# The last round of a hybrid decoder by 272 and 240 tokens, with a fixed order of both norms' work

## The chip, the cores and the metric

The kernel runs on one core of one Trainium2 chip. The metric is the device time of one execution in microseconds (us). A core has five engines that run their own instruction queues in order: TensorE (PE, with its weight loads PEld), VectorE (DVE), ScalarE (ACT), GpSimd (POOL) and SyncE (SP, which here issues DMAs only). They wait for one another by semaphores.

## The reference

Two layers of a decoder trunk. Each is an RMSNorm, one projection for two groups of heads (attention with forgetting, and retention), an output projection with a residual add, then a second RMSNorm and a SwiGLU feed-forward block with a residual add. 16 learned meta tokens stand before the 512 real ones and are dropped at the end, after a final RMSNorm.

```python
def rmsnorm(x, g):
    x32 = x.astype(jnp.float32)
    y = x32 * lax.rsqrt(jnp.mean(x32 * x32, axis=-1, keepdims=True) + EPS)
    return (y * g.astype(jnp.float32)).astype(x.dtype)
...
    hn = rmsnorm(h, ffn_norm_g)
    ff = jax.nn.silu(jnp.einsum('bld,df->blf', hn, w_gate)) * jnp.einsum('bld,df->blf', hn, w_up)
    return h + jnp.einsum('blf,fd->bld', ff, w_down)
...
    for i in range(DEPTH):
        h = hybrid_layer(h, ...)
    h = rmsnorm(h, final_norm)
    return h[:, N_META:]
```

D_MODEL is 1024, the feed-forward width 2816, everything float32.

## The kernel before

**Layout.** The residual stream is eight tiles `h[0]` to `h[7]`, each 128 features by 528 tokens (16 meta and 512 real); the second layer computes its feed-forward block for the 512 real tokens alone, columns 16 to 528. Each weight block of 128 features by up to eight blocks is fetched by SP, and split on the chip into a high part (`whi`, `fwhi`, rounded to fp32r) and a low part (`wlo`, `fwlo`); activations are split the same way (`ah`, `al`). A product is then three fp32r matmuls: high by high, low by high, high by low.

**The feed-forward block** (`ffn`) goes in rounds over the 22 blocks of the hidden width (`ROUNDS`); each round's part of the down projection is added to `h` (`down`). The last round has three hidden blocks (n = 3). In the second layer (`last`) its down projection is written out in `ffn` itself, from `add_part` on: the tokens go in two parts, `LC`, of 320 and 192 columns, and for each part the eight feature blocks m one after the other. One such product is 3 x 3 = 9 matmuls into one bank of PSUM (`psum_a`, four banks in turn), and `add_part` (L1010) adds the bank to `h[m]` on VectorE.

**The final norm** needs the sum over all 1024 features of the squares, so over all eight tiles. For the first part `squares` (L308 to L314) squares each tile on ScalarE and sums the squares on VectorE, `col_parts` splits the sum into a high and a low part (`sqh`, `sql`, L128, L129), and `col_rstd` multiplies both by a matrix of ones on TensorE (L273), which sums over the 128 partitions and spreads the result. From it come 1/rms by a logarithm (L278) and an exponential (L279) on ScalarE and one Newton step of three instructions on VectorE (L280, L282, L283). `scaled` (L1066) multiplies each tile by the norm's weight on ScalarE, `final` (L1053) multiplies two tiles at a time by 1/rms on VectorE and has SP write them out (L1056). For the second part `squares_last` (L323 to L336) does the same with the squares of the last two tiles going to the sums by themselves: tile 6 as float32, tile 7 split into two.

**Order.** A list of steps, `steps`, is put together first and then run; `merge` puts the steps in `places` between those of `rnd` by the index of a product's step (`end` is the end of the first part). TensorE's instructions stand in exactly this order. The instructions of the other engines are ordered by a scheduler, except those that `tc.keep_in_program_order` pins; `tc.high_priority` moves others forward. Before, `places` has ten entries: all of the first part's squares and scalings behind its last product, its 1/rms nine steps later (behind the third product of the second part), everything else behind the last product:

```python
            LC = ((t0, t0 + 320), (t0 + 320, T))
...
            places = [(end, lambda: squares(fin[0], LC[0:1])),
                      (end + 9, lambda: rstd(fin[0], LC[0:1], "r")),
                      (end + 9, lambda: scaled(fin[0], *LC[0], 0, NK)),
                      (2 * end, lambda: scaled(fin[1], *LC[1], 0, NK - 1)),
...
                      (2 * end, lambda: final(fin[1], *LC[1], 0, NK))]
```

GpSimd does subtractions of the weight splits in the attention stages (L177) and nothing after them.

Of the kernel before, what the change touches and what calls it, by code (L numbers as in the profile page):

```python
# [10 lines left out]
F32 = mybir.dt.float32  # L11
F32R = mybir.dt.float32r
AF = mybir.ActivationFunctionType
ALU = mybir.AluOpType

D = 1024
NK = D // 128
SEQ = 512
META = 16
T = SEQ + META  # L20
# [8 lines left out]
HB = NK // 2  # L29
EPS = 1e-6  # L30
# [8 lines left out]
def hybrid_kernel(ctx, tc, x_t, w_in, w_fl, w_out, w_gate, w_up, w_down, vecs, b_fg, rope, decay, mask, ident, out_t):  # L39
    nc = tc.nc  # L40
# [9 lines left out]
    h = [state.tile([128, T], F32, name=f"h{k}") for k in range(NK)]  # L50
# [9 lines left out]
    ones = const.tile([128, 128], F32R, name="ones")  # L60
    nc.vector.memset(ones.bitcast(F32), 1.0)
    epsc = const.tile([128, 1], F32, name="epsc")
# [64 lines left out]
    def split(hi, lo, src):  # L127
        nc.scalar.copy(hi, src)  # L128
        nc.vector.tensor_sub(lo, src, hi.bitcast(F32))  # L129
# [109 lines left out]
    def psum():  # L239
        return psd.tile([128, 2, 512], F32, name="psd", tag="psd")  # L240

    def psum_a():
        return psa.tile([128, 512], F32, name="psa", tag="psa")
# [5 lines left out]
    def tt(name, dt=F32):  # L249
        tag, bufs = tags[name]  # L250
        return tmp.tile([128, T], dt, name=name, tag=tag, bufs=bufs)
# [4 lines left out]
    def fft(tag, dt=F32R, shape=(128, T), bufs=None):  # L256
        return phase["ffn"].tile(list(shape), dt, name=tag, tag=tag, bufs=bufs)

    def col_parts(src, cols):
        c_all = slice(cols[0][0], cols[-1][1])  # L260
        sh = tt("sqh", F32R)
        sl = tt("sql", F32R)
        split(sh[:, c_all], sl[:, c_all], src[:, c_all])
        return sh, sl

    def col_rstd(parts, n, cols, rname):


        c_all = slice(cols[0][0], cols[-1][1])
        views = [psum_a()[:, 0:c1 - c0] for c0, c1 in cols]  # L270
        for i, s in enumerate(parts):
            for v, (c0, c1) in zip(views, cols):
                nc.tensor.matmul(v, ones if s.dtype == F32R else ones.bitcast(F32), s[:, c0:c1], start=(i == 0), stop=(i == len(parts) - 1))  # L273
        with tc.high_priority():
            r = tt(rname)
            a = tt("nwt")
            for v, (c0, c1) in zip(views, cols):
                nc.scalar.activation(r[:, c0:c1], v, AF.Ln, bias=epsc, scale=1.0 / n)  # L278
            nc.scalar.activation(r[:, c_all], r[:, c_all], AF.Exp, scale=-0.5)  # L279
            nc.vector.tensor_mul(a[:, c_all], r[:, c_all], r[:, c_all])  # L280
            for v, (c0, c1) in zip(views, cols):
                nc.vector.scalar_tensor_tensor(a[:, c0:c1], v, n * EPS, a[:, c0:c1], ALU.add, ALU.mult)  # L282
            nc.vector.scalar_tensor_tensor(r[:, c_all], a[:, c_all], 3.0 * n, r[:, c_all], ALU.subtract, ALU.mult)  # L283
        return r
# [18 lines left out]
    def squares(st, cols, pinned=False):  # L303
        c = slice(cols[0][0], cols[-1][1])
        acc = tt("ss")
        for k in range(NK):
            if k == 0:
                first = nc.scalar.activation(acc[:, c], h[0][:, c], AF.Square)  # L308
                if pinned:
                    tc.keep_in_program_order(first)  # L310
            else:
                sq = tt("sq")
                nc.scalar.activation(sq[:, c], h[k][:, c], AF.Square)
                nc.vector.tensor_add(acc[:, c], acc[:, c], sq[:, c])  # L314
        st["parts"] = col_parts(acc, cols)

    def squares_last(st, cols):

        c = slice(*cols[0])
        acc = tt("ss")  # L320
        for k in range(NK - 2):
            sq = tt("sq") if k else acc
            nc.scalar.activation(sq[:, c], h[k][:, c], AF.Square)  # L323
            if k:
                with tc.high_priority():
                    nc.vector.tensor_add(acc[:, c], acc[:, c], sq[:, c])
        hi, lo = col_parts(acc, cols)
        one = fft("S", F32, (128, T), 2)
        t = fft("tl1", shape=(128, 2, T))
        sh, sl = t[:, 0], t[:, 1]  # L330
        sq = tt("sq")
        nc.scalar.activation(one[:, c], h[NK - 2][:, c], AF.Square)
        nc.scalar.activation(sh[:, c], h[NK - 1][:, c], AF.Square)
        with tc.high_priority():
            nc.vector.tensor_mul(sq[:, c], h[NK - 1][:, c], h[NK - 1][:, c])
            nc.vector.tensor_sub(sl[:, c], sq[:, c], sh[:, c].bitcast(F32))  # L336
        st["parts"] = (hi, one, lo, sh, sl)

    def rstd(st, cols, rname="R"):

        st["R"] = col_rstd(st["parts"], D, cols, rname)
# [394 lines left out]
    def ffn(l, st, real, last):  # L736
        QC = REAL if real else FULL
        t0 = META if real else 0
        w = (T - t0) // 2
# [90 lines left out]
        class Unit:  # L830
# [42 lines left out]
            def bank(self, n):  # L873
                def go():
                    if n not in self.t:
                        if n == "x":
                            self.t["x"] = psum_a()
                        else:
                            ps = self.t["zy"] = psum()
                            self.t["z"], self.t["y"] = ps[:, 0], ps[:, 1]  # L880
                    return self.t[n]
                return go
# [89 lines left out]
        for r, (f0, f1) in enumerate(ROUNDS):  # L972
            for f in range(f0, f1):
# [12 lines left out]
                if fills:  # L986
                    p, g0, g1 = fills.pop(0)
# [12 lines left out]
        n = f1 - f0  # L1000
        js = [down_job(p, f0, f1) for p, _, _ in fills]
        if not last:
            for p in range(NK // 2):
                for s in range(2):
                    steps += down(js[p], s, 2 * p + s, f0, f1, False)
        else:

            def add_part(m, c0, c1, bank):
                def go():
                    nc.vector.tensor_add(h[m][:, c0:c1], bank()[:, 0:c1 - c0], h[m][:, c0:c1])  # L1010
                return go

            rnd = []
            LC = ((t0, t0 + 320), (t0 + 320, T))
            for c0, c1 in LC:
                for m in range(NK):
                    ps = []

                    def bank(ps=ps):
                        if not ps:  # L1020
                            ps.append(psum_a())
                        return ps[0]

                    rnd += product(js[m // 2], m % 2 * n, lambda k, c0=c0, c1=c1: [t[:, c0:c1] for t in acts[f0 + k]],
                                   bank, True, True, n, add_part(m, c0, c1, bank))
            fin = [{}, {}]
            end = NK * n
            places = [(end, lambda: squares(fin[0], LC[0:1])),
                      (end + 9, lambda: rstd(fin[0], LC[0:1], "r")),
                      (end + 9, lambda: scaled(fin[0], *LC[0], 0, NK)),  # L1030
                      (2 * end, lambda: scaled(fin[1], *LC[1], 0, NK - 1)),
                      (2 * end, lambda: squares_last(fin[1], LC[1:2])),
                      (2 * end, lambda: final(fin[0], *LC[0], HB, NK)),
                      (2 * end, lambda: scaled(fin[1], *LC[1], NK - 1, NK)),
                      (2 * end, lambda: final(fin[0], *LC[0], 0, HB)),
                      (2 * end, lambda: rstd(fin[1], LC[1:2], "R")),
                      (2 * end, lambda: final(fin[1], *LC[1], 0, NK))]
            steps += merge(rnd, places)
        for i in range(HB):
            steps.insert(NK + 4 + 9 * i, x_forms(i))  # L1040
# [4 lines left out]

    gf = const.tile([128, NK], F32, name="gf")
    nc.vector.tensor_scalar_mul(gf, vec[:, V_FIN:V_FIN + NK], RSC)

    def final(st, c0, c1, k0, k1):
        r = st["R"][:, c0:c1].unsqueeze(1).broadcast_to([128, 2, c1 - c0])  # L1050
        for k in range(k0, k1, 2):
            y = st["y"][k // HB][:, k % HB:k % HB + 2]
            mul = nc.vector.tensor_mul(y, y, r)  # L1053
            if k0:
                tc.keep_in_program_order(mul)
            nc.sync.dma_start(out_t[k:k + 2, :, c0 - META:c1 - META].rearrange("k p c -> p k c"), y)  # L1056

    def scaled(st, c0, c1, k0, k1):
        if k0 == 0:
            if c0 == META:  # L1060
                st["y"] = [fft(f"th{i}", F32, (128, HB, c1 - c0)) for i in range(2)]
            else:
                y = fft("tl0", F32, (128, NK, c1 - c0))
                st["y"] = [y[:, 0:HB], y[:, HB:NK]]
        for k in range(k0, k1):
            y = nc.scalar.activation(st["y"][k // HB][:, k % HB], h[k][:, c0:c1], AF.Copy, scale=gf[:, k:k + 1])  # L1066
            if k0:
                tc.keep_in_program_order(y)

    def layer(l):  # L1070

# [155 lines left out]
```

## Time and profile before

| | us |
|---|---|
| median of 3 runs | 1300.8 (1298.96 to 1301.67) |
| the profiled execution | 1302.07 |
| its span, first to last instruction | 1300.3 |

The profile is of one execution. Its first page gives the span, the busy time of each engine and the costliest groups of instructions; further views give the busy time in windows, the instructions in order of time, and the chain of waits: from the last instruction back to what released it at each step. A row of the timeline has the start, the duration, the engine, the line of the kernel, the operation, what is written from what, the shape, a count of merged instructions, and in brackets how long the engine was idle before and what ended that. `h<-psa,h` is the residual add, `th<-h,gf` and `tl<-h,gf` are the scalings of the first and second part, `ss<-ss,sq` the summing of squares, `tl<-tl,R` the products with 1/rms of the second part. SPq is SP's queue of DMA issues.

### The profile page before, as it was taken

How to read it: one execution, taken by the hardware profiler on the slowest of the kernel's cores; microseconds unless marked ns; L12 is line 12 of the kernel's file. 1: busy time of each engine (PE TensorE's matmuls, PEld its weight loads, DVE VectorE, ACT ScalarE, POOL GpSimd, SP SyncE). 2: the span in 40 equal slices, each digit the busy share in tenths (PEclk: the TensorE clock that was granted, in tenths of full speed). 3: DMA queues.
4: the chain of work that ended last, by engine and by line, in shares of the span. 5: the costliest groups of instructions: out<-in, count | busy, mean ns of one | idle time of the engine just before them, and what ended most of it. 6: DMA issues, size and time to landing. Idle time of an engine off the chain costs nothing.

```text
span 1300.3 us, 23291 instructions
## 1 busy us (share of the span) xinstructions
PE 1271.6 (98%) x9326; PEld 1210.3 (93%) x9326; DVE 1005.5 (77%) x1827; ACT 706.7 (54%) x1277; POOL 192.7 (15%) x157
## 2 busy tenths in 40 slices
PE   8999999999999999999999999999999999999996
PEld 7999999999999999999998989988789999999995
DVE  7877756869988777777786767568899888888866
ACT  6776555576444444444466665457764444444444
POOL 3332333230000000000013324333200000000000
PEclk9999899999999999999999999999999999999998
DMA  5322222213333333332323222222224333333321
GB/s 196 107 76 72 74 82 82 60 55 122 103 110 98 98 98 98 98 98 82 102 71 115 74 82 82 77 87 66 97 81 129 99 98 97 98 111 103 96 65 65
DMA packets 45468, 120.54 MB, mean 93 GB/s; under 512 B 5376, under 2 KB 12032, under 8 KB 45360
## 3 DMA queue, kind: packets, MB, share of 16 engines
q1 hardware_dynamic: 45120, 118.90, 29.1%
q8 instruction: 73, 1.20, 0.4%
q14 instruction: 35, 0.29, 0.1%
q0 software_dynamic: 96, 0.13, 0.1%
q10 hardware_dynamic: 144, 0.02, 0.0%
HBM read 116.91 MB, written 2.13 MB: 92 GB/s over the span
## 4 chain that ended last, share of the span: by engine, by line
PE 82%; DVE 9%; ACT 6%; issue 1%; DMA 1%; POOL 0%; SPq 0%; DVEq 0%; ACTq 0%; POOLq 0%
PE psd L200 23%; PE psa L823 17%; PE psd L958 14%; PE psd L823 13%; PE psa L200 5%; PE psa L958 4%; PE psa L396 2%; PE psa L480 1%; PE psa L687 1%; PE psa L540 1%; DVE xl L299 1%; ACT whi L176 1%; PE psa L657 1%; DVE tq L585 1%; DVE ptl L129 1%
## 5 line engine op out<-in xcount | busy, mean ns | idle before, releaser
L177 POOL TENSOR_TENSOR wlo<-raw,whi 128x512 fp32r<-128x512 f32 x136 | 186.8, 1388 | 399.5 <-ACT whi L176 396.6
L200 PE MATMUL psd<-xh,whi 128*128 128x264 f32 (+1 forms) x792 | 198.0, 318 | 5.1 <-ACT whi L176 4.7
L200 PE MATMUL psd<-xh,wlo 128*128 128x264 f32 (+1 forms) x792 | 188.1, 305 | 0.4 <-POOL wlo L177 0.4
L200 PE MATMUL psd<-xl,whi 128*128 128x264 f32 (+1 forms) x792 | 188.0, 305 | 0.0
L200 PEld LDWEIGHTS psd<-xh,whi 128*128 128x128 f32 x792 | 130.2, 192 | 9.6 <-ACT whi L176 4.7
L200 PEld LDWEIGHTS psd<-xh,wlo 128*128 128x128 f32 x792 | 128.7, 191 | 6.5 <-POOL wlo L177 0.6
L200 PEld LDWEIGHTS psd<-xl,whi 128*128 128x128 f32 x792 | 129.3, 191 | 4.2 <-DVE xl L299 0.3
L176 ACT CAST whi<-raw 128x512 fp32r<-128x512 f32 (+1 forms) x170 | 99.6, 613 | 34.4 <-issue 17.8
L811 ACT CAST whi<-raw 128x1024 fp32r<-128x1024 f32 (+2 forms) x62 | 54.9, 885 | 49.8 <-PE psd L823 37.5
L811 ACT CAST fwhi<-raw 128x1024 fp32r<-128x1024 f32 (+2 forms) x62 | 55.7, 898 | 47.4 <-PE psd L823 39.7
L812 DVE TENSOR_TENSOR wlo<-raw,whi 128x1024 fp32r<-128x1024 f32 (+2 forms) x62 | 62.8, 1013 | 11.5 <-ACT whi L811 11.4
L812 DVE TENSOR_TENSOR fwlo<-raw,fwhi 128x1024 fp32r<-128x1024 f32 (+2 forms) x62 | 63.9, 1031 | 9.0 <-ACT fwhi L811 8.6
L823 PE MATMUL psa<-tl,whi 128*128 128x264 f32 (+1 forms) x232 | 65.8, 284 | 0.0
L823 PE MATMUL psa<-th,whi 128*128 128x264 f32 (+1 forms) x232 | 65.8, 284 | 0.0
L823 PE MATMUL psa<-th,wlo 128*128 128x264 f32 (+1 forms) x232 | 65.7, 283 | 0.0
L823 PE MATMUL psa<-th,fwhi 128*128 128x264 f32 (+1 forms) x224 | 63.6, 284 | 0.0
L823 PE MATMUL psa<-th,fwlo 128*128 128x264 f32 (+1 forms) x224 | 63.5, 283 | 0.0
L823 PE MATMUL psa<-tl,fwhi 128*128 128x264 f32 (+1 forms) x224 | 63.4, 283 | 0.0
L499 ACT ACTIVATE pdNone<-pdNone,nmax 128x144 f32<-128x144 f32 (+1 forms) x64 | 37.0, 577 | 47.9 <-DVE nmax L486 35.7
L129 DVE TENSOR_TENSOR ptl<-psa,pth 128x512 fp32r<-128x512 f32 (+4 forms) x88 | 41.8, 490 | 23.3 <-ACT pth L128 23.1
L811 ACT CAST fwhi<-S 128x1024 fp32r<-128x1024 f32 x20 | 21.0, 1051 | 69.7 <-PE psa L823 66.3
L889 ACT COPY e<-psa 128x264 f32<-128x264 f32 (+1 forms) x114 | 42.8, 375 | 27.7 <-PE psa L823 23.8
(311 smaller groups left out, 4035.7 us busy)
## 6 DMA issues: line engine op xcount, KB each, us to landing
raw<-w_in SPq DMA_DIRECT2D x54, 512.0 KB, 3.5
raw<-w_gate SPq DMA_DIRECT2D x44, 512.0 KB, 3.9
fraw<-w_up SPq DMA_DIRECT2D x38, 512.0 KB, 3.5
raw<-w_down SPq DMA_DIRECT2D x64, 256.0 KB, 2.9
raw<-w_out SPq DMA_DIRECT2D x16, 512.0 KB, 3.6
raw<-w_down SPq DMA_DIRECT2D x32, 192.0 KB, 2.5
bc<-cdr SPq DMA_DIRECT2D x16, 264.0 KB, 3.5
raw<-w_up SPq DMA_DIRECT2D x6, 512.0 KB, 3.4
```

What stands on the lines that cost most here:

```text
L129: nc.vector.tensor_sub(lo, src, hi.bitcast(F32))
L176: nc.scalar.copy(hi, job["raw"][:, c0:c1])
L177: sub(lo, job["raw"][:, c0:c1], hi.bitcast(F32))
L200: nc.tensor.matmul(ps[1][b][:, 0:c1 - c0], w[:, wk, :], x[:, c0:c1], start=(k == 0 and i == 0), stop=(k == n - 1 and i == 2))
L299: nc.vector.scalar_tensor_tensor(xl[:, c], h[k][:, c], g, xh[:, c].bitcast(F32), ALU.mult, ALU.subtract)
L396: nc.tensor.transpose(ps[:, 128 * j:128 * j + 128], src[:, o:o + 128], idt)
L499: nc.scalar.activation(pr, pr, AF.Exp, bias=nmax[0:nq], scale=-1.0, accum_out=rsum)
L811: nc.scalar.copy(hi, src)
L812: nc.vector.tensor_sub(lo, src, hi.bitcast(F32))
L823: nc.tensor.matmul(bank()[:, 0:b.shape[-1]], a[:, o + k, :], b, start=(fresh and k == 0 and i == 0), stop=(k == n - 1 and i == 2), skip_gr ...
L889: nc.scalar.copy(self.t["e"][:, i], self.t["x"][:, 0:w])
L958: nc.tensor.matmul(v[:, 0:c1 - c0], a[:, s * n + k, :], b[:, c0:c1], start=(k == 0 and i == 0), stop=(k == n - 1 and i == 2))
```

## The change

The functions `squares_last`, `final` and `scaled` go. The last round's tokens are parted by 272 and 240 (`PA`, `PB`). What follows each product of the second part is written out by hand in `after_0` to `after_7`, and nearly all of it is pinned to that order on VectorE and ScalarE; `after_a` follows the first part's last product. 1/rms of the first part is computed between the products of the second (`root` on ScalarE in `after_2`, `newton` on VectorE in `after_3` and `after_4`). The squares of the second part's tiles 1 to 4 are added to that of tile 0 as before; those of tiles 5, 6 and 7 go to the sums on TensorE as float32 by themselves, so five operands are summed: three in float32, and the high and the low part of the sum of tiles 0 to 4. The products with 1/rms of the first part's tiles 0 to 3 (two instructions of 544 columns) and of the second part's tiles 6 and 7 (one of 480) are on GpSimd, the other five on VectorE. The order of SP's output DMAs is: first part 0, 2, 4, 6, then second part 6, 0, 2, 4.

```diff
-            LC = ((t0, t0 + 320), (t0 + 320, T))
-            for c0, c1 in LC:
+            PA, PB = (t0, t0 + 272), (t0 + 272, T)
+            ca, cb = slice(*PA), slice(*PB)
+            na, nb = PA[1] - PA[0], PB[1] - PB[0]
+            fin = {}
...
+                    f = nc.vector.tensor_add(h[m][:, c0:c1], bank()[:, 0:c1 - c0], h[m][:, c0:c1])
+                    if c0 > t0:
+                        pin(f)
...
+            for c0, c1 in (PA, PB):
...
-            fin = [{}, {}]
+            def scale_a(m):
+                nc.scalar.activation(fin["ya"][m // HB][:, m % HB], h[m][:, ca], AF.Copy, scale=gf[:, m:m + 1])
+
+            def scale_b(*ms):
+                for m in ms:
+                    pin(nc.scalar.activation(fin["yb"][:, m], h[m][:, cb], AF.Copy, scale=gf[:, m:m + 1]))
+
+            def square_b(m):
+                if m == 0:
+                    t = fft("S", F32, (128, 6, w), 2)
+                    fin["one"] = [t[:, i, 0:nb] for i in range(3)]
+                    fin["acc"], fin["rb"], fin["tb"] = (t[:, i, 0:nb] for i in range(3, 6))
+                    d = fin["acc"]
+                elif m < NK - 3:
+                    fin["sq", m] = d = tt("sq")[:, 0:nb]
+                else:
+                    d = fin["one"][m - NK + 3]
+                pin(nc.scalar.activation(d, h[m][:, cb], AF.Square))
+
+            def sum_b(m):
+                pin(nc.vector.tensor_add(fin["acc"], fin["acc"], fin["sq", m]))
+
+            def out(eng, y, r, k, c0, c1):
+                pair = r.unsqueeze(1).broadcast_to([128, 2, c1 - c0])
+                f = eng.tensor_mul(y, y, pair)
+                if eng is nc.vector:
+                    pin(f)
+                nc.sync.dma_start(out_t[k:k + 2, :, c0 - META:c1 - META].rearrange("k p c -> p k c"), y)
+
+            def out_a(eng, k):
+                out(eng, fin["ya"][k // HB][:, k % HB:k % HB + 2], fin["ra"], k, *PA)
+
+            def out_b(eng, k):
+                out(eng, fin["yb"][:, k:k + 2], fin["rb"], k, *PB)
+
+            def root(r, v):
+                pin(nc.scalar.activation(r, v, AF.Ln, bias=epsc, scale=1.0 / D))
+                pin(nc.scalar.activation(r, r, AF.Exp, scale=-0.5))
+
+            def newton(i, r, v, a):
+                if i == 0:
+                    pin(nc.vector.tensor_mul(a, r, r))
+                elif i == 1:
+                    pin(nc.vector.scalar_tensor_tensor(a, v, D * EPS, a, ALU.add, ALU.mult))
+                else:
+                    pin(nc.vector.scalar_tensor_tensor(r, a, 3.0 * D, r, ALU.subtract, ALU.mult))
+
+            def sums(v, parts):
+                for i, t in enumerate(parts):
+                    nc.tensor.matmul(v, ones if t.dtype == F32R else ones.bitcast(F32), t, start=(i == 0), stop=(i == len(parts) - 1))
+
+            def after_a():
...
+                for m in range(NK):
+                    sq = tt("sq") if m else acc
+                    nc.scalar.activation(sq[:, ca], h[m][:, ca], AF.Square)
+                    if m:
+                        nc.vector.tensor_add(acc[:, ca], acc[:, ca], sq[:, ca])
+                    scale_a(m)
+                hi, lo = tt("sqh", F32R), tt("sql", F32R)
+                nc.scalar.copy(hi[:, ca], acc[:, ca])
...
+            def after_0():
+                hi, lo, acc = fin["a"]
+                pin(nc.vector.tensor_sub(lo, acc, hi.bitcast(F32)))
+                square_b(0)
+
+            def after_1():
+                square_b(1)
+
+            def after_2():
+                fin["va"] = psum_a()[:, 0:na]
+                sums(fin["va"], fin["a"][0:2])
...
+                root(fin["ra"], fin["va"])
+                sum_b(1)
+                square_b(2)
+
+            def after_3():
+                a = fin["ra"], fin["va"], fin["ta"]
+                sum_b(2)
+                newton(0, *a)
+                newton(1, *a)
+                square_b(3)
+                scale_b(0, 1)
+
+            def after_4():
+                newton(2, fin["ra"], fin["va"], fin["ta"])
+                sum_b(3)
+                square_b(4)
+                scale_b(2)
+                out_a(nc.gpsimd, 0)
+                out_a(nc.gpsimd, 2)
+
+            def after_5():
+                sum_b(4)
+                scale_b(3)
+                square_b(5)
+                hi, lo = tt("sqh", F32R)[:, 0:nb], tt("sql", F32R)[:, 0:nb]
+                pin(nc.scalar.copy(hi, fin["acc"]))
+                fin["b"] = hi, lo
+
+            def after_6():
+                square_b(6)
+
+            def after_7():
+                hi, lo = fin["b"]
+                pin(nc.vector.tensor_sub(lo, fin["acc"], hi.bitcast(F32)))
+                square_b(7)
+                scale_b(4)
+                v = psum_a()[:, 0:nb]
+                sums(v, (fin["one"][0], hi, fin["one"][1], lo, fin["one"][2]))
+                root(fin["rb"], v)
+                out_a(nc.vector, 4)
+                out_a(nc.vector, 6)
+                scale_b(5, 6, 7)
+                for i in range(3):
+                    newton(i, fin["rb"], v, fin["tb"])
+                out_b(nc.gpsimd, 6)
+                for k in (0, 2, 4):
+                    out_b(nc.vector, k)
+
             end = NK * n
-            places = [(end, lambda: squares(fin[0], LC[0:1])),
...
+            places = [(end, after_a)] + [(end + n * (i + 1), f) for i, f in enumerate(
+                (after_0, after_1, after_2, after_3, after_4, after_5, after_6, after_7))]
```

More of the change, by code (lines that the diff above doesn't have):

```diff
@@ L315, in squares @@
         st["parts"] = col_parts(acc, cols)
[L317 to L337, printed above, removed]
     def rstd(st, cols, rname="R"):
@@ L1006, in ffn, with pin @@
         else:
+            def pin(f):
+                tc.keep_in_program_order(f)
+            PA, PB = (t0, t0 + 272), (t0 + 272, T)
+            ca, cb = slice(*PA), slice(*PB)
+            na, nb = PA[1] - PA[0], PB[1] - PB[0]
+            fin = {}
             def add_part(m, c0, c1, bank):
                 def go():
-                    nc.vector.tensor_add(h[m][:, c0:c1], bank()[:, 0:c1 - c0], h[m][:, c0:c1])
+                    f = nc.vector.tensor_add(h[m][:, c0:c1], bank()[:, 0:c1 - c0], h[m][:, c0:c1])
+                    if c0 > t0:
+                        pin(f)
                 return go
             rnd = []
-            LC = ((t0, t0 + 320), (t0 + 320, T))
-            for c0, c1 in LC:
+            for c0, c1 in (PA, PB):
                 for m in range(NK):
@@ L1025, in ffn @@
                                    bank, True, True, n, add_part(m, c0, c1, bank))
-            fin = [{}, {}]
-            end = NK * n
-            places = [(end, lambda: squares(fin[0], LC[0:1])),
[L1029 to L1037, printed above, removed]
+            def scale_a(m):
+                nc.scalar.activation(fin["ya"][m // HB][:, m % HB], h[m][:, ca], AF.Copy, scale=gf[:, m:m + 1])
@@ new lines, in sums @@
+            def sums(v, parts):
+                for i, t in enumerate(parts):
+                    nc.tensor.matmul(v, ones if t.dtype == F32R else ones.bitcast(F32), t, start=(i == 0), stop=(i == len(parts) - 1))
+            def after_a():
+                fin["ya"] = [fft(f"th{i}", F32, (128, HB, na)) for i in range(2)]
+                fin["yb"] = fft("tl0", F32, (128, NK, nb))
+                acc = tt("ss")
+                for m in range(NK):
[6 more added lines that the diff above has]
+                nc.scalar.copy(hi[:, ca], acc[:, ca])
+                fin["a"] = (hi[:, ca], lo[:, ca], acc[:, ca])
@@ new lines, in after_0 @@
+            def after_0():
[7 more added lines that the diff above has]
+                sums(fin["va"], fin["a"][0:2])
+                fin["ra"], fin["ta"] = (fft("e", F32, (128, T), 2)[:, 0:na] for _ in range(2))
+                root(fin["ra"], fin["va"])
+                sum_b(1)
+                square_b(2)
@@ L1047, in hybrid_kernel @@
     nc.vector.tensor_scalar_mul(gf, vec[:, V_FIN:V_FIN + NK], RSC)
[L1049 to L1068, printed above, removed]
     def layer(l):
```

## The prediction

> **What bounds the kernel now.** I read the page first, then the windows by stage, then the chain of waits, and the timelines only of the last 35 us: the compiled instructions of both kernels are the same on every engine, with the same waits, up to the last round, so only that stretch can change.
>
> ```profile
> span 1300.3 us, 23291 instructions
> PE 1271.6 (98%) x9326; PEld 1210.3 (93%) x9326; DVE 1005.5 (77%) x1827; ACT 706.7 (54%) x1277; POOL 192.7 (15%) x157
> ```
>
> ```profile
> 1286.50:1289.60 3.10, 0.00 (x0) 0.00 (x0) 1.17 (x4) 1.76 (x5) 0.00 (x0) 1.00 0.30 111
> 1289.60:1296.20 6.60, 2.13 (x6) 1.64 (x6) 5.63 (x14) 2.09 (x7) 0.00 (x0) 0.50 0.27 99
> 1296.20:1298.70 2.50, 0.00 (x0) 0.00 (x0) 0.48 (x2) 0.00 (x0) 0.00 (x0) 0.50 0.95 312
> ```
>
> TensorE bounds the kernel at 98% of the span, but not its end. The columns of the windows are PE, PEld, DVE, ACT, POOL, granted clock, DMA share and GB/s. TensorE has no matmul between 1286.5 and 1289.6, only six matmuls, the sums of the norm, after that, and from 1296.2 to 1298.7 only the output moves, with the DMA engines at 95%. The last 13.8 us are a tail of VectorE, ScalarE and DMA. The chain of waits says what they wait for:
>
> ```profile
> 1286.42 0.28 DVE h L1010
> 1286.70 0.02 issue
> 1286.73 0.45 ACT tl L1066
> 1287.18 0.26 ACT sq L323
> 1287.44 0.02 issue
> 1287.46 0.36 DVE ss L326
> 1287.82 0.28 DVE h L1010
> ...
> 1290.00 0.28 DVE h L1010
> ...
> 1291.06 1.61 PE psa L273 x5
> ...
> 1294.32 0.37 DVE R L283
> ```
>
> From residual add to residual add it is a round of 1.40 us (1286.42 to 1287.82): add, scaling on ScalarE, square, sum on VectorE, next add. VectorE executes in order, so the next piece's add, whose product has long been ready, queues behind the sum of the piece before it. The last add ends at 1290.28, 3.8 us after the last product, and 1/rms of the second part (call its end R) is there at 1294.69.
>
> **The change: TensorE.** First the spacing of matmuls by width, from windows that hold one width each (columns PE, PEld, clock, DMA):
>
> ```profile
> 1245.23:1252.36 7.13, 7.13 (x60) 7.08 (x59) 1.00 0.37 111
> 1266.26:1276.82 10.56, 10.56 (x72) 10.56 (x72) 1.00 0.00 0
> 1276.82:1279.81 2.99, 2.99 (x29) 2.98 (x27) 1.00 0.02 5
> 1279.81:1280.28 0.47, 0.16 (x2) 0.00 (x1) 1.00 0.00 0
> ```
>
> 256 columns: 60 in 7.13 us, 0.119 each. 320: 72 in 10.56, 0.147. 192: 27 loads in 2.99, 0.111 (two matmuls of the wider run still end in the window). Between them 272 costs 0.125 and 240 about 0.115. The fourth window holds the two sums of part A's norm, 0.47. Part A then takes 72 x 0.125 = 9.0 and ends at 1275.3; part B 72 x 0.115 = 8.3, with 0.47 for those sums in its middle: the last product ends near 1284.2 instead of 1286.5. No bank holds it up: the bank of part A's sums is read by `newton(1)` near 1281.6, and needed near 1282.
>
> **The fixed order on VectorE and ScalarE.** Durations, by shape:
>
> ```profile
> L1010 DVE TENSOR_TENSOR h<-psa,h 128x320 f32<-128x320 f32 x8 | 3.9, 484 | 1.1 <-PE psa L823 1.1
> L1010 DVE TENSOR_TENSOR h<-psa,h 128x192 f32<-128x192 f32 x8 | 2.5, 348 | 0.0
> ```
>
> ```profile
> L1066 ACT ACTIVATE th<-h,gf 128x320 f32<-128x320 f32 x8 | 4.4, 549 | 0.0
> L1066 ACT ACTIVATE tl<-h,gf 128x192 f32<-128x192 f32 x8 | 3.5, 450 | 4.1 <-DVE h L1010 4.1
> L323 ACT ACTIVATE sq<-h 128x192 f32<-128x192 f32 x5 | 1.6, 349 | 0.0
> L278 ACT ACTIVATE R<-psa,epsc 128x192 f32<-128x192 f32 x1 | 0.4, 420 | 1.1 <-PE psa L273 1.1
> L279 ACT ACTIVATE R<-R 128x192 f32<-128x192 f32 x1 | 0.4, 363 | 0.0
> ```
>
> VectorE needs 1.06 ns a column: 0.44 for 272, 0.405 for 240, 0.65 for 480; the next one on the engine can start 0.08 before the end (the chain counts the add of 0.348 as 0.28), one on another engine 0.02 after it (the "issue" rows). ScalarE needs 0.8 ns a column more: at 240 0.49 for a scaling, 0.39 for a square, 0.46 for the logarithm, 0.40 for the exponential. In the new order a piece's add no longer stands behind its predecessor's scaling; three squares go to the sums unadded (three f32 operands in place of one; TensorE has room), and part A's last two scalings are behind the last add. `squares_last` goes with its extra multiply and subtraction.
>
> Part A: add 0.44, square 0.43, sum 0.36 and two hand-overs make 1.3 us a piece against 1.13 of products, but two of its adds stand ahead of earlier sums in the built order, so its last sum ends near 1276.9 and its rounded copy at 1277.4. Its two sums on TensorE stand behind the third product of B, at 1275.3 + 27 x 0.115 = 1278.4; until then 1 us of cover, so part A's norm costs nothing, and a late copy would hold up all later products.
>
> Part B by the same durations: sums drained at 1279.0, logarithm and exponential 0.9 more: 1279.95. Add 3 starts at 1280.06 when its product is there, then sum 2 and two of the three `newton` steps to 1281.6, add 4 to 1281.9, the third step at 1282.26, sum 3 at 1282.58, add 5 at 1282.9. All adds would follow the products if GpSimd did not come in here.
>
> **The products on GpSimd.** Each has two SBUF operands (tile and 1/rms). This trace shows what that does to VectorE:
>
> ```profile
> L177 POOL TENSOR_TENSOR wlo<-raw,whi x136: 1272/1293/2378, 25.6 to 929.3; 128x512 fp32r<-128x512 f32 x136
> ```
>
> ```profile
> 75.99 1.30 POOL L177 TENSOR_TENSOR wlo<-raw,whi 128x512 fp32r<-128x512 f32 x1 [2.40 <-ACT whi L176]
> 77.53 1.35 POOL L177 TENSOR_TENSOR wlo<-raw,whi 128x512 fp32r<-128x512 f32 x1 [0.24 <-ACT whi L176]
> ```
>
> ```profile
> 75.88 0.69 DVE L407 SCALAR_TENSOR_TENSOR tq<-psd,R 128x528 f32<-128x528 f32 x1
> 76.54 1.20 DVE L129 TENSOR_TENSOR rsl<-sd,rsh 128x416 fp32r<-128x416 f32 x1
> 77.66 1.25 DVE L129 TENSOR_TENSOR rs<-sd,rs 16x16 fp32r<-16x16 f32 x1
> ```
>
> ```profile
> 30.22 2.38 POOL L177 TENSOR_TENSOR wlo<-raw,whi 128x512 fp32r<-128x512 f32 x1
> ```
>
> ```profile
> 30.75 0.69 DVE L1082 SCALAR_TENSOR_TENSOR cr<-cr,R 128x528 f32<-128x528 f32 x1
> ```
>
> A 16-column operation of VectorE took 1.25 us: it ended at 78.91, just after GpSimd's at 78.88. The one of 416 columns ended at 77.74, 0.45 after GpSimd's at 77.29, which is its bare streaming at 1.06 ns a column. With two SBUF operands the two engines take turns; the one with an operand in PSUM (75.88, 0.69 beside GpSimd's from 75.99) passes freely, so the adds are free and sums, `lo` and products are not. When GpSimd was already waiting as a VectorE operation ended, it was mostly next (77.53: before the 16 columns queued behind 76.54); in the 30.22 row VectorE went on with the next one, to 31.44, and GpSimd ended 1.16 after that, at 32.60.
>
> The multiply with a repeated operand is not in the trace. Bounds: 1 to 1.5 times the subtraction's 1.16 of 512 columns, as it keeps two operands but walks another pattern; I take 1: 1.23 for 544 columns, 1.09 for 480. The first product starts at 1282.58 and ends at 1283.81. Sum 4, due at 1282.83, waits and ends at 1284.08; adds 6 and 7 queue behind it and end at 1284.4 and 1284.7. The second product runs from 1284.08 to 1285.31, and `lo` of part B, due at 1284.6, ends at 1285.58. TensorE needs it for the fourth sum; with the f32 one behind it and the drain that is 1286.35 (estimate 0.75, from 1.61 for five at half clock). Logarithm, exponential and three `newton` steps: 0.45 + 0.40 + 3 x 0.405 and gaps of 0.03: **R near 1288.6**, 6.1 earlier. Part A's last products on VectorE (0.65 each, from 1285.5) fit under the logarithm. The three scalings behind the exponential on ScalarE (3 x 0.39) end near 1288.5, 0.1 before R. Both follow the exponential, so that cover of 0.1 moves along; each 0.1 beyond it would hold tile 6 back by as much.
>
> The GPSIMD Engine Reference of the Trainium skill (Key points) says the same against this change: GpSimd shares its SBUF interfaces with VectorE and contends with instructions that have two SBUF inputs; without it the sum would be the first rival's. TensorE: Matmul & The Clock Gate (Part 1, The HAM clock gate) has the clock fall to half after an idle window of about 3.4 us; the windows above agree (0.50 from 1289.6, 3.1 after the last product). The gaps here stay under 1 us, so the sums should run at full clock; at half they would cost some 0.4 more, 1296.8 in all.
>
> **After R** VectorE takes tile 0 (1288.63 to 1289.28), GpSimd tile 6 (to 1290.37), VectorE tiles 2 and 4 (to 1291.5). SP's queue holds tile 6 first, so tile 0 waits there for GpSimd though it is done; part A's four outputs stand ahead of it, issued from 1283.9 to 1286.9 and landed by 1289.5, so they cost nothing. The queue of before:
>
> ```profile
> 1295.34 1.97 SPq L1056 DMA_DIRECT2D out_t<-tl  x4
> out_t<-tl SPq DMA_DIRECT2D x4, 192.0 KB, 2.2
> 1294.00:1295.00 1.00, 0.00 (x0) 0.00 (x0) 0.93 (x3) 0.00 (x0) 0.00 (x0) 0.50 0.97 365
> ```
>
> Issue at 1295.34, data from 1296.2, engines full until 1298.7, end 1.6 later. Now: issue at 1290.45, data from 1291.35; four times 240 KB at 312 to 365 GB/s (rows of 768 bytes in the last window, of 1280 here), I take 335, need 2.93 instead of 2.5: until 1294.28; plus 1.6: **1295.9**. So R gains 6.1 and the tail behind it gives back 1.7 (1.2 for the wait on GpSimd, 0.5 for wider rows): net 4.4 us. The profiled execution took 1302.07 with a span of 1300.3, 1.3 above the median 1300.8 of the three runs; the median becomes 1300.8 - 4.4 = **1296.4**.
>
> **The rivals.** *GpSimd and VectorE run side by side.* `lo` ends at 1284.9, the last square at 1285.0, R is 1287.85, tile 6 is issued near 1289.2, and the span ends near 1294.65: 1295.2. For it: nothing but the untried pattern; against it: every row above. 12%.
>
> *VectorE keeps its turn after R.* Its three products run through (to 1290.45), GpSimd ends at 1291.54, SP issues tile 6 at 1291.6, and everything ends at 1297.05: 1297.6. For it: the 30.22 row. Against it: 77.53. 13%.
>
> *The multiply on GpSimd is slow.* All three stand in series on the way to the end, 3.55 us together; at k times the price the end moves by 3.55 (k - 1). At k = 2.25 the gain is gone, from k = 3 it is slower by over 0.2%; at 3.3 it is 1304.6. For it: no row has a multiply or a repeated operand. Against it: 136 rows of the same operand count with a median of 1293 ns. 5% slower, and 8% near no change, to which I also count that the order buys nothing because another wait on ScalarE takes its place.
>
> **How the numbers follow.** Forecast 62%, rivals 12, 13, 8 and 5. About 0.2%, 2.6 us, can be told from no change (the three runs lie 2.7 apart). Faster by more: 62 + 12 + 13 = 87%. Range 1294.5 (first rival, less scatter) to 1298.5 (second rival, or k = 1.5, 1298.2).
>
> **What would show it.** Right: the last product near 1284.2; sum 4 and `lo` over 0.7 us long, ending with GpSimd's products; products of 1.2 to 1.5 us; R near 1288.6; clock 1.0 in the sums; tile 6 as the first output behind R, 1.8 after it; DMA full for about 2.9. Wrong: sums on VectorE at their bare 0.4 beside GpSimd (first rival), tile 6 after tile 4 (second), or products above 2.5 us (third).

## The result and the profile after

| | before | after |
|---|---|---|
| median of six runs each, us | 1300.41 (1298.96 to 1302.43) | 1295.28 (1294.01 to 1295.55) |
| ratio, 95% interval | | 0.9961 [0.9951, 0.9971] |
| profiled execution, us | 1302.07 | 1295.23 |

The changed kernel is 5.1 us faster by the medians; 4.4 was forecast. The head of its page:

```profile
span 1293.5 us, 23290 instructions
PE 1268.8 (98%) x9328; PEld 1207.2 (93%) x9328; DVE 1005.5 (78%) x1821; ACT 706.9 (55%) x1277; POOL 197.3 (15%) x160
```

The spans differ by 6.8, more than the change is worth. The timeline of each kernel shows why, at the first matmul of its last round (columns: start, duration, engine, line). Before:

```profile
1266.26 0.31 PE L823 MATMUL psa<-ah,whi 128*128 128x320 f32 x1
```

After:

```profile
1264.31 0.29 PE L801 MATMUL psa<-ah,whi 128*128 128x272 f32 x1
```

Up to here the instructions are the same, and yet 1.95 us have gone: scatter between executions (in the runs below this matmul comes anywhere from 1262.8 to 1266.9, behind the same instructions). From here on every moment is therefore counted from this matmul, written with a plus; profiled times of different kernels then compare to a few hundredths. The windows of after, from the last matmuls to the outputs (PE, PEld, DVE, ACT, POOL, granted clock, DMA share, GB/s):

```profile
1281.60:1284.20 2.60, 2.38 (x10) 1.11 (x8) 2.60 (x6) 1.47 (x5) 1.41 (x1) 1.00 0.39 140
1284.20:1286.40 2.20, 0.00 (x0) 0.00 (x0) 1.57 (x4) 1.97 (x5) 0.00 (x0) 1.00 0.97 333
1286.40:1288.95 2.55, 0.00 (x0) 0.00 (x0) 2.54 (x3) 0.00 (x0) 1.60 (x1) 0.60 0.02 7
1289.00:1291.50 2.50, 0.00 (x0) 0.00 (x0) 0.20 (x1) 0.00 (x0) 0.00 (x0) 0.50 1.03 338
```

The sums now start right behind the products, at full clock (before, 3.2 us behind them, at 0.50). The chain of waits of after names what is left (DVEq is VectorE's sequencer, where the next instruction stands):

```profile
1280.55 1.26 DVE S L1035
1281.81 0.63 DVE h L997 x2
1282.44 0.85 DVE sql L1125
1283.29 0.04 issue
1283.33 0.80 PE psa L1064 x3
...
1284.15 0.47 ACT S L1051
1284.62 0.02 issue
1284.65 0.41 ACT S L1052
...
1285.97 0.42 DVE S L1060
1286.38 0.02 issue
1286.41 0.66 DVE tl L1039
1287.07 1.57 DVEq L1306
1288.63 0.57 DVE tl L1039
```

The first and third rows are two-operand instructions of 240 columns that took 1.26 and 0.85 where 0.4 is their bare time, and the row of 1.57 is a VectorE that could not go on; GpSimd's rows in the timeline of after stand beside them:

```profile
1280.16 2.85 POOL L1039 TENSOR_TENSOR th<-th,e 128x544 f32<-128x544 f32 x2 [351.06 <-ACT sq L1032]
...
1282.36 0.92 DVE L1125 TENSOR_TENSOR sql<-S,sqh 128x240 fp32r<-128x240 f32 x1
...
1286.52 1.60 POOL L1039 TENSOR_TENSOR tl<-tl,S 128x480 f32<-128x480 f32 x1 [3.51 <-DVE S L1060]
```

Where the time came from, in moments behind the first matmul of the last round:

| | before | after | gain |
|---|---|---|---|
| last product ends | +20.20 | +17.47 | 2.73 |
| from there to R (1/rms of the second part) | 8.22 | 4.60 | 3.62 |
| from R to the end | 5.58 | 7.09 | -1.51 |
| end of the span | +34.00 | +29.16 | 4.84 |

Not all of the first row is the new widths. In the last round of the kernel before, TensorE had itself stood still for an add that had to empty a bank, as its waits in that profile show (who waited for what: us in total, times, longest); after, it has no such wait:

```profile
PE psa L823 <- DVE h L1010: 0.7, 1, 0.7
```

### The profile page after: what moved, and what is told of

The parts are those of the page before. It is cut to its first block, busy times and chain, and to the rows that moved or that the text cites. A ratio compares the mean times of both kernels' runs of the same rounds, so it can differ in the third digit from the quotient of the medians.

```text
span 1293.5 us, 23290 instructions
## 1 busy us (share of the span) xinstructions
PE 1268.8 (98%) x9328; PEld 1207.2 (93%) x9328; DVE 1005.5 (78%) x1821; ACT 706.9 (55%) x1277; POOL 197.3 (15%) x160
## 4 chain that ended last, share of the span: by engine, by line
PE 83%; DVE 9%; ACT 6%; issue 1%; DMA 1%; POOL 0%; DVEq 0%; SPq 0%; ACTq 0%; POOLq 0%
PE psd L200 23%; PE psa L801 18%; PE psd L936 14%; PE psd L801 13%; PE psa L200 5%; PE psa L936 4%; PE psa L374 2%; PE psa L458 1%; PE psa L518 1%; DVE tq L563 1%; PE psa L635 1%; ACT whi L176 1%; DVE xl L299 1%; PE psa L665 1%; DVE ptl L129 1%
## 5 line engine op out<-in xcount | busy, mean ns | idle before, releaser
L176 ACT CAST whi<-raw 128x512 fp32r<-128x512 f32 (+1 forms) x170 | 99.7, 613 | 34.4 <-issue 17.8
```

What stands on the lines that cost most here:

```text
L176: nc.scalar.copy(hi, job["raw"][:, c0:c1])
```

## The experiments

The theory: the fixed order (with the unadded squares) makes R earlier by some 6 us, and the three multiplications on GpSimd only cost time; the new split adds a little. The rivals: the split does it, or GpSimd helps by taking work off VectorE.

**The split alone**, on the kernel before:

```diff
-            LC = ((t0, t0 + 320), (t0 + 320, T))
+            LC = ((t0, t0 + 272), (t0 + 272, T))
```

> The kernel before with its last round by 272 and 240 instead of 320 and 192, nothing else. Times are counted from the first matmul of the last round to the end of the span: 34.0 us in the kernel before, 29.2 in the changed one. Theory (the order makes the gain: an add no longer queues behind the sum of the piece before it): the first norm comes 2.0 earlier, every later round of add, scaling, square and sum is 0.13 longer and the output 0.5: 33.4, a gain of 0.6. Rival (the split makes the gain, as the products end 2.7 earlier): 31.3 or less.

Median 1300.13, ratio 0.9995 [0.9985, 1.0004]; end at +34.33. No gain at all, so the rival that the split does it is out; but the theory's +33.4 is missed too, by 0.9. The waits of TensorE and the timeline of this kernel show where it went:

```profile
PE psa L823 <- DVE h L1010: 1.3, 1, 1.3
```

```profile
1278.43 0.44 DVE L280 TENSOR_TENSOR nwt<-r 128x272 f32<-128x272 f32 x1 [1.36 <-ACT r L279]
...
1280.82 0.72 DVE L1053 TENSOR_TENSOR th<-th,r 128x544 f32<-128x544 f32 x1
...
1281.77 0.40 DVE L1010 TENSOR_TENSOR h<-psa,h 128x240 f32<-128x240 f32 x1
1282.21 0.50 ACT L1066 ACTIVATE tl<-h,gf 128x240 f32<-128x240 f32 x1 [1.95 <-DVE h L1010]
```

The scheduler put part A's Newton step and two of its output multiplications ahead of the fourth add of part B. The add empties a PSUM bank; until 1282.17 TensorE had none free and stood still for 1.3 us. The last product came at +19.05 and not near +17.9, and R (+28.26) 0.16 earlier than before.

**The order alone**, the changed kernel with the old widths:

```diff
-            PA, PB = (t0, t0 + 272), (t0 + 272, T)
+            PA, PB = (t0, t0 + 320), (t0 + 320, T)
```

> The changed kernel with its last round by 320 and 192 as before, so the new order and GpSimd without the new split. Theory (order): products end near +19.1 instead of +17.5, part A's GpSimd products are 0.2 longer each, the second part's steps 0.05 shorter each, its output 0.4 shorter: 1/rms of the second part at +23.5, end at +30.1 (3.9 of the 4.8 gained). Rival (split): the gain shrinks to what is left without the earlier products, end at +32 or later.

Median 1296.16, ratio 0.9969 [0.9958, 0.9981], end at +30.33: 3.67 of the 4.84 are the order's (with the unadded squares and GpSimd, which this kernel has too). Its last product ends at +19.17, so of the 2.73 in the table 1.03 come from the order as well. The split is worth the other 1.17 at the end, and only under the new order: the two are not a sum.

**The order not pinned**, all else as changed:

```diff
             def pin(f):
-                tc.keep_in_program_order(f)
+                pass
```

> The changed kernel without the pins: the scheduler orders VectorE and ScalarE. In the order that it builds, the second part's adds 3 to 7 stand behind part A's newton steps and two of its products, and sum 4 and lo before adds 5 to 7. Theory (order): add 3 starts near +18 instead of +13.5, 1/rms of the second part comes near +27, end near +34: the whole gain is gone. Rival (split): most of the gain stays, end at +30 or earlier.

Median 1302.0, ratio 1.0017 [1.0007, 1.0027]: slower than before, end at +35.49, R at +28.40. So what counts is the pinned order. Its timeline has the same late add as the split alone, with GpSimd now making it later:

```profile
1283.01 2.49 DVE L1039 TENSOR_TENSOR th<-th,e 128x544 f32<-128x544 f32 x2
...
1283.15 3.57 POOL L1039 TENSOR_TENSOR th<-th,e 128x544 f32<-128x544 f32 x2 [351.45 <-DVE e L1060]
...
1285.88 0.38 PE L801 MATMUL psa<-ah,fwhi 128*128 128x240 f32 x1 [2.04 <-DVE h L997]
```

Its windows show the sums back at half clock:

```profile
1287.10:1289.50 2.40, 0.06 (x1) 0.00 (x0) 1.47 (x5) 1.28 (x4) 0.00 (x0) 0.79 0.79 273
1289.50:1291.60 2.10, 1.75 (x6) 1.56 (x6) 0.49 (x2) 2.04 (x6) 0.00 (x0) 0.50 0.25 86
```

The expectation (R near +27, end near +34) is missed by 1.4 and 1.5, so the miss lies ahead of R; from R to the end it is 7.08, as expected and as in the changed kernel. Of the 1.4, 0.5 is add 3, which started at +18.5 and not near +18. The expectation has nothing on the clock of the sums, whose eight matmuls, at 0.50, are one piece of the chain of waits:

```profile
1289.85 3.21 PE psa L1064 x8
```

Against the kernel before, R is the same (+28.40, +28.42), and the loss is the longer end behind it (5.58 before).

**The unadded squares taken back**: squares 5 and 6 of part B are added on VectorE, and three operands go to the sums in place of five. (`square_b` keeps a tile of its own for the last square alone; the rounded copy and `lo` move behind the last sum.)

```diff
             def after_6():
+                sum_b(5)
                 square_b(6)
...
             def after_7():
+                sum_b(6)
...
-                sums(v, (fin["one"][0], hi, fin["one"][1], lo, fin["one"][2]))
+                sums(v, (hi, fin["one"][0], lo))
```

> The changed kernel, but with only the last square going to the sums unadded: squares 5 and 6 of the second part are added on VectorE, and the sums take three operands in place of five. Theory (the unadded squares take work off the path to the sums): sum 5, with two SBUF operands, waits for GpSimd's second product and ends near +18.95, sum 6 at +19.6, the rounded copy at +20.0, lo at +20.4, 1/rms near +23.1 in place of +22.07, end +30.2. Rival (the fixed order alone does it, the unadded squares only move time to TensorE): 1/rms within 0.2 of +22.07, end +29.0 to +29.4.

Median 1296.48, ratio 0.9977 [0.9968, 0.9986]; R at +23.41, end at +30.51. The unadded squares are worth 1.35 in the traces. The timeline of this kernel shows two sums that waited for GpSimd, and a `lo` that did not:

```profile
1279.85 2.83 POOL L1039 TENSOR_TENSOR th<-th,e 128x544 f32<-128x544 f32 x2 [351.11 <-ACT sq L1032]
...
1280.23 1.25 DVE L1035 TENSOR_TENSOR S<-S,sq 128x240 f32<-128x240 f32 x1
1281.41 0.39 DVE L997 TENSOR_TENSOR h<-psa,h 128x240 f32<-128x240 f32 x1
1281.72 1.22 DVE L1035 TENSOR_TENSOR S<-S,sq 128x240 f32<-128x240 f32 x1
...
1284.03 0.41 DVE L1125 TENSOR_TENSOR sql<-S,sqh 128x240 fp32r<-128x240 f32 x1 [0.46 <-ACT sqh L1124]
```

So there is no third wait for GpSimd: the second has moved from `lo` (0.92 in the changed kernel, 0.41 here) to sum 5. Sum 4 ends at +17.49 here and +17.50 there, but `lo` only at +20.45 and not at +18.97, because sums 5 and 6 and the rounded copy (`sqh`, for which VectorE stands idle for the 0.46 in brackets) now come one after the other between them.

**Without GpSimd**: all products on VectorE, part A's four behind `lo`, part B's in the order 0, 2, 4, 6.

```diff
-                out_a(nc.gpsimd, 0)
-                out_a(nc.gpsimd, 2)
...
+                out_a(nc.vector, 0)
+                out_a(nc.vector, 2)
...
-                out_b(nc.gpsimd, 6)
-                for k in (0, 2, 4):
+                for k in (0, 2, 4, 6):
```

> The changed kernel with all products by 1/rms on VectorE: the first part's tiles 0 and 2 behind its tiles 4 and 6, the second part's in the order 0, 2, 4, 6, and SP's queue in the same order. Theory (GpSimd and VectorE take turns, and SP's queue waits for GpSimd's tile): sum 4 and lo take 0.4 each (1.26 and 0.92 in the changed kernel), the sums end 0.8 earlier, VectorE fills that with the two products, so 1/rms comes at the same +22.0; the first output behind it is issued 0.7 after it and not 1.8: end at +28.1, 1.0 faster than the changed kernel. Rival (GpSimd takes work off VectorE): three more products on VectorE make it 1 to 2 us slower than the changed kernel, +30.2 or later.

Median 1294.71, ratio 0.9952 [0.9937, 0.9967], end at +28.04. The same sum 4 and `lo`, without GpSimd beside them, are in the timeline of this kernel:

```profile
1281.48 0.40 DVE L1035 TENSOR_TENSOR S<-S,sq 128x240 f32<-128x240 f32 x1
...
1283.08 0.40 DVE L1123 TENSOR_TENSOR sql<-S,sqh 128x240 fp32r<-128x240 f32 x1
1283.40 2.62 DVE L1039 TENSOR_TENSOR th<-th,e 128x544 f32<-128x544 f32 x4
```

0.40 and 0.40 in place of 1.26 and 0.92. That settles what GpSimd does to them. But `lo`, 0.74 earlier (+18.23 against +18.97), made R only 0.09 earlier (+21.98): the four products of 2.62 behind it now stand before part B's Newton step.

**Only tile 6 of part B on VectorE**, as the last:

```diff
-                out_b(nc.gpsimd, 6)
-                for k in (0, 2, 4):
+                for k in (0, 2, 4, 6):
```

> The changed kernel with the second part's tiles 6 and 7 multiplied on VectorE as the last of four, and SP's queue in that order; the first part's tiles 0 to 3 stay on GpSimd. Theory: 1/rms of the second part stays at +22.1, the first output is issued 0.7 after it instead of 1.8: end at +28.1. Rival: the fourth product on VectorE adds its 0.57: +29.7.

Median 1293.96, ratio 0.9949 [0.9933, 0.9966]; R unchanged at +22.07, end at +28.14. Tile 6 on GpSimd, as the first of part B in SP's queue, costs 1.02 at the end.

**All on VectorE, part A's tile 0 at once**: as in the last edit, and part A's tile 0 multiplied right behind that part's 1/rms, its other three behind `lo`.

```diff
-                out_a(nc.gpsimd, 0)
-                out_a(nc.gpsimd, 2)
+                out_a(nc.vector, 0)
...
-                out_a(nc.vector, 4)
-                out_a(nc.vector, 6)
+                for k in (2, 4, 6):
+                    out_a(nc.vector, k)
```

> All products on VectorE as in the run without GpSimd, but the first part's tile 0 at once behind part A's last newton step, in a gap that VectorE has between the adds, and tiles 2, 4, 6 behind lo. Theory: sum 4 ends 0.2 earlier than in the changed kernel, lo ends at +18.2 (18.97 there), three products of 0.64 end as the exponential does, 1/rms comes at +21.5: end at +27.6, 1.6 faster than the changed kernel. Rival (GpSimd takes work off VectorE): +30 or later.

Median 1293.21, ratio 0.9949 [0.9934, 0.9963]; R at +21.53, end at +27.60, as expected. From its timeline, with `lo` at its bare time and the four products one after the other:

```profile
1280.60 0.40 DVE L1124 TENSOR_TENSOR sql<-S,sqh 128x240 fp32r<-128x240 f32 x1
...
1284.33 2.36 DVE L1039 TENSOR_TENSOR tl<-tl,S 128x480 f32<-128x480 f32 x4
1285.05 2.04 SPq L1042 DMA_DIRECT2D out_t<-tl  x4
```

**The wait in SP's queue.** GpSimd keeps tile 6, but the code names tile 0 first:

> The changed kernel with one thing moved: the output of the second part's tile 0 stands before that of tile 6 in SP's queue (0, 6, 2, 4 instead of 6, 0, 2, 4); the engines keep their products. Theory: tile 0 is issued 0.7 after 1/rms while GpSimd is still at tile 6, the DMA engines start 1.1 earlier but then wait for tile 2: end at +28.5 (29.2 in the changed kernel, 34.0 before). Rival (the output is bound by the last product, not by the queue): +29.2.

Median 1295.61, end at +29.18, the changed kernel's. It tells nothing of the queue: the scheduler orders SP's transfers by itself, and the compiled queue still held tile 6 ahead of tile 0. So the edit was made again with the transfers pinned:

```diff
-                nc.sync.dma_start(out_t[k:k + 2, :, c0 - META:c1 - META].rearrange("k p c -> p k c"), y)
+                d = nc.sync.dma_start(out_t[k:k + 2, :, c0 - META:c1 - META].rearrange("k p c -> p k c"), y)
+                if c0 > t0:
+                    pin(d)
...
+                out_b(nc.vector, 0)
                 out_b(nc.gpsimd, 6)
-                for k in (0, 2, 4):
+                for k in (2, 4):
```

> As s5, but with the four last output transfers pinned too, so that SP's queue really holds tile 0, 6, 2, 4 (in s5 the compiled queue kept tile 6 ahead of tile 0, as in the changed kernel, so s5 was the changed kernel once more). Times from the first matmul of the last round; the changed kernel's 1/rms of the second part is there at +22.07, its first output behind that at +23.84, its end at +29.16. Theory (the wait for GpSimd's tile in SP's queue holds back the data): first output at +22.8, tile 6 at +23.85, DMA data from +23.7, last data 0.65 earlier, end +28.5. Rival (the end is set by VectorE's last tile, or GpSimd's lock, and not by the queue): first output at +22.8 too, but the end at +29.1 or later.

Median 1294.29, ratio 0.996 [0.9945, 0.9975], end at +28.50. SP's waits in the execution without the pin:

```profile
SPq L1042 <- POOL tl L1039: 3.1, 1, 3.1
```

and with it:

```profile
SPq L1042 <- DVE tl L1039: 2.1, 1, 2.1
...
SPq L1042 <- POOL tl L1039: 0.6, 1, 0.6
```

The first output behind R moved from +23.84 to +22.82. The queue's order is worth 0.66, and the instructions of the engines are the same.

**The two ends beside each other** on one chip, the changed kernel and the one with all on VectorE, each as it was:

> The changed kernel itself, as the one that the others of this call stand beside: end at +29.1 to +29.2 after the first matmul of the last round, ratio to the kernel before 0.996.

> The kernel of s7 (no scaling on GpSimd, the first part's tile 0 scaled on VectorE right behind that part's 1/rms) beside the changed kernel on one chip: end +27.6 against +29.16, so 1.6 us faster than the changed kernel in the profiled executions, and a median 1.0 to 2.2 lower (the spread between executions, about 2 us, blurs it). Rival (the earlier difference was scatter): median within 0.5 of the changed kernel's.

1295.53 (1294.55 to 1296.25, six runs), ratio 0.9966 [0.9954, 0.9978], and 1293.11 (1292.29 to 1293.66, four runs), ratio 0.9948 [0.9931, 0.9964]; ends at +29.17 and +27.59. Every run of the second lies below every run of the first. The version without GpSimd beats both kernels: 2.4 us under the changed one by these medians, a little more than the 1.0 to 2.2 expected, 1.58 in the traces.

## Why the prediction was right

Predicted 1296.4, measured 1295.28, inside the range. Of the 1.1 between them 0.4 is the net in the traces (4.84, not 4.4) and 0.4 the median before (1300.41 by six runs, not 1300.8); the rest is within the scatter of the medians. By its steps (its times less 1266.26, the first matmul of its last round):

| step | predicted | measured |
|---|---|---|
| last product | +17.9 | +17.47 |
| sum 4 ends | +17.8 | +17.50 |
| `lo` ends | +19.3 | +18.97 |
| from `lo` to the end of the sums | 0.75 | 0.84 |
| R | +22.3 | +22.07 |
| first output behind R, after R | 1.8 | 1.77 |
| R earlier by | 6.1 | 6.35 |
| given back behind R | 1.7 | 1.51 |
| DMA engines full for | 2.93 | 2.9 |
| net | 4.4 | 4.84 |

The last product came 0.47 earlier than forecast, and R only 0.23: the sums wait for `lo`, not for the last product.

- **TensorE.** Right but for sizes, which these windows of after show (part A, then part B with the two sums of part A's norm):

```profile
1264.31:1273.34 9.03, 9.03 (x74) 9.03 (x73) 6.40 (x14) 5.76 (x13) 0.00 (x0) 1.00 0.00 0
1273.34:1281.78 8.44, 8.44 (x76) 8.44 (x76) 7.00 (x18) 6.58 (x17) 1.62 (x2) 1.00 0.01 2
```

9.0 was forecast for the first and 8.3 + 0.47 for the second, where two terms were too large. The matmuls of 240 columns follow each other at 0.112, the 192-column ones of before at 0.111, so the 0.115 between 320 and 192 was too much. And from the first of the two sums to the next product it is 0.25 here:

```profile
1276.32 0.29 PE L1064 MATMUL psa<-sqh,ones 128*128 128x272 f32 x1
...
1276.57 0.28 PE L801 MATMUL psa<-ah,fwhi 128*128 128x240 f32 x1
```

The 0.47 is right for the kernel before (the 0.16 busy in its row counts L823 alone, and the sums are L273). It goes with the old widths: 0.45 with them under the new order, 0.26 with the new ones under the old order. With the old widths the second sum started 0.05 after its operand `sql` was done, with the new ones 0.5 after; that this makes the difference was not tested.
- **The fixed order.** Right, and the heart of the gain: pinned, with the old widths, 3.67; not pinned, a loss. The forecast did not say that the split is worth something only with it, which the split alone showed (0.0).
- **Turns on SBUF.** Right, on both of its counts: sum 4 and `lo` over 0.7 long with GpSimd, each ending 0.27 behind the GpSimd product beside it, and 0.40 without. The first rival (side by side) falls. So does the second: behind R VectorE had tile 0, GpSimd tile 6, then VectorE again, which is the 1.57 in the chain.
- **The multiply's price.** Forecast 1.23 and 1.09, the subtraction's price per column. The sign announced was 1.2 to 1.5 from start to end. Tile 6 took longer, 1.60 (timeline above); part A's two took 1.38 and 1.51, with a mean just inside, in the groups of after (instructions | busy us, mean ns of one | idle before):

```profile
L1039 POOL TENSOR_TENSOR th<-th,e 128x544 f32<-128x544 f32 x2 | 2.8, 1445 | 351.1 <-ACT sq L1032 351.1
```

All three include waits for a turn. Net, tile 6 could begin when VectorE's tile 0 was done (1287.07) and ended at 1286.52 + 1.60 = 1288.12: 1.05 for 480 columns, just under the forecast. The third rival falls.
- **Behind R.** 1.7 forecast, 1.2 for the wait and 0.5 for wider rows; 1.51 measured. The runs separate the two: with the new widths and no GpSimd behind R it is 6.07 from R to the end, in the split alone (+28.26 to +34.33) and in the version all on VectorE (+21.53 to +27.60), so 0.49 for the wider part and 1.02 for GpSimd. Of this 1.02 the order in SP's queue makes 0.66. No run takes the other 0.36 apart; with tile 0 first in the queue, tiles 2 and 4 still stand behind GpSimd's turn.
- **The clock.** The sums ran at 1.00, as forecast.

The forecast priced the products on GpSimd as a loss within a gain, and the runs agree: with all on VectorE the last round ends 6.40 earlier than before, in place of 4.84.

## What to carry to other kernels

At the end of a kernel that TensorE bounds, the order of small instructions on an in-order engine can matter more than how TensorE's work is cut: pin the adds that empty PSUM banks ahead of anything that could wait, and only then look for the best widths. Moving elementwise products with two SBUF operands to GpSimd saved nothing here: each took nearly twice VectorE's time, and VectorE, which had such work of its own, waited it out. Where VectorE does them counts too: behind `lo`, they cost it almost what GpSimd's turns did (R 0.09 earlier); with one of them in a gap between the adds, R came 0.54 earlier. And look in the compiled queue, not in the code, for which transfer stands ahead of which: a transfer that waits for the slowest producer holds back those that are ready.

## What the runs showed of the hardware

The turn is by whole instruction: a sum of 240 columns waits out what is left of a GpSimd instruction of some 1.4 us (1.26 in place of 0.40 here), while adds with an operand in PSUM took their usual 0.39 to 0.40 in the middle of GpSimd's stretch (the row from 1281.41 above). The clock fell a little sooner than in the kernel before. The windows of after by the microsecond:

```profile
1286.00:1287.00 1.00, 0.00 (x0) 0.00 (x0) 0.96 (x3) 0.20 (x1) 0.48 (x1) 0.96 0.47 165
1287.00:1288.00 1.00, 0.00 (x0) 0.00 (x0) 1.00 (x2) 0.00 (x0) 1.00 (x1) 0.50 0.00 0
```

A mean of 0.96 between 1.00 and 0.50 puts the fall 0.08 before 1287.00, which is 2.8 us after the last matmul (1283.33 + 0.80 = 1284.13, in the chain of after); the prediction found some 3.1 before. TensorE: Matmul & The Clock Gate of the Trainium skill (Part 1, The HAM clock gate) has one idle window of about 3.4 us; 2.8 and 3.1 are less. The other runs show that the lag is not one number, nor one of the kernel: with the same instructions on TensorE it was 2.8, 3.4, 3.0 and 3.1 (the changed kernel, the queue order not pinned, the changed kernel again, the queue order pinned), and without GpSimd 4.5, where the last matmul ended at 1284.32 and this window puts the fall at 1288.84:

```profile
1288.00:1289.00 1.00, 0.00 (x0) 0.00 (x0) 1.00 (x3) 0.00 (x0) 0.00 (x0) 0.92 0.33 115
```

In the order not pinned, TensorE stood still for 2.0 us, worked for 1.3 and stood still again, and the clock fell 1.3 after that second stop. So the time since the last matmul does not say when the clock falls. What sets it, the runs leave open.
